# A hybrid mixer layer on one core: the output projection with pairs of token tiles, seven products of quarters in place of eight

## The chip, the cores and the metric

The kernel runs on one core of a Trainium2 chip. Its time is the device time of one execution in microseconds (us); the times given are those of repeated executions on the same inputs. Five engines work side by side: TensorE (PE: matmuls; PEld is its weight load), VectorE (DVE), ScalarE (ACT), GpSimd (POOL) and SyncE (SP), which here only issues transfers. Each engine runs its own instructions in the order written out for it, and a wait at the head of that order holds back everything behind it.

## The reference

One layer for two requests: a prompt of 128 tokens and a sample of 2048 (2176 in all, 17 tiles of 128), model width 1024. All arithmetic is float32:

```python
xn = rmsnorm(h, ln_g) * (1.0 + scale) + shift
proj = jnp.einsum('btd,de->bte', xn, w_in)            # three mixers, their gates, three merge gates
br = jnp.stack([o_a, o_b, o_c], axis=2)               # delta net, spatial gating, Fourier: 512 wide each
pb = jnp.einsum('btnw,nwd->btnd', br, w_branch)
gt = jax.nn.sigmoid(gates.reshape(B, T, N_BRANCH, D_MODEL))
merged = jnp.einsum('btnd,btnd->btd', gt, pb)
out = jnp.einsum('btd,de->bte', merged, w_out)        # the out-projection
h = h + gate * out                                    # gate: a part of the adaLN modulation
y = rmsnorm(h, final_g)
```

The change touches the last three lines and the loading of `w_out`.

## The kernel before

Every float32 operand of a large product is scaled by a power of two and split in two float16 parts, hi and lo; a product is three matmuls (hi x hi, hi x lo, lo x hi) that accumulate in one PSUM bank. The power of two comes from a sum of squares: ACT squares the operand (L209 for weights, L1464 for merged tiles), DVE casts the sum (L175), PE adds it over the partitions with one matmul of one column against `ones`, DVE makes the scale with five one-column steps (L183 to L187, L220), ACT writes the high part (L222, L1466) and DVE the low part (L223, L1467).

The last part of the program has four stages. merge(1), merge(2) and merge(0) each handle one branch: for eight column blocks of 128 (db 0 to 7) and, in each, token tiles of 512, 512, 128 (upper half) and 512, 512 (lower half), PE computes the gate's 24 matmuls and the branch's 12; ACT takes the sigmoid (L1389), DVE multiplies (L1398), POOL adds onto the merged rows (L1399), which are read from and written back to DRAM (`mrg`: load L1377 on SP, store L1406 on POOL). Weights for the next db are loaded by `read_w` (L195) into the staging buffer `wst`. It has two copies (`bufs=2`), and the gate weights (w_in), W_branch, the adaLN rows for the output gate (`gate_rows`, L1421, summed by DVE on L386) and W_out all go through those two. merge(0) is the last: in it, one block of W_out per db is loaded, scaled by itself, and split into `wohi` and `wolo` by `out_w`.

Then comes the out-projection, 17 token tiles in the order 16, 8 to 15, 0 to 7. `out_prep` (L1453 to L1470) loads a tile of merged rows, squares, scales and splits it, and, since each column block of W_out has its own scale, makes eight inverse scales (L1469) with which POOL scales the gate's row per tile (L1489). Per tile and half of the columns, 24 matmuls (L161: token tile as the stationary operand, 512 columns of W_out as the moving one) fill a bank; DVE multiplies by the gate (L1524), POOL adds the input row (L1525), ACT squares (L1534), POOL takes the power (L171), DVE multiplies by the final norm (L1537), and the row is stored (L1538). PSUM has three banks for these products (`ps_mm`), three others (`ps_d`) served the delta net.

The order on each engine is set by the framework, which moves instructions by priority and by what it expects to be ready; `high_priority` lifts a piece of code over what was written before it. The operands of the first five tiles, `pre`, are made when merge(0)'s last upper half is done (`ahead_out`).

Of the kernel before, what the change touches and what calls it, by code (L numbers as in the profile page):

```python
# [111 lines left out]
def hybrid_flow_kernel(ctx: ExitStack, tc: tile.TileContext, x_prompt, x_sample, state_delta, c, c_ctx, ln_g, w_ada,  # L112
# [1340 lines left out]
    def out_prep(t, pl, tag, hl=None):  # L1453
        mt = sb(pl, [P, KT, P], tag, bufs=2)
        SY.dma_start(mt, mD[:, :, t * P:(t + 1) * P].rearrange("k p t -> p k t"))
        if hl is None:
            mh = sb(orp, [P, KT, P], "mh", F16, bufs=3)
            ml = sb(orp, [P, KT, P], "ml", F16, bufs=3)
        else:
            mh = sb(wp, [P, KT, P], "whi", F16, bufs=4)  # L1460
            ml = sb(wp, [P, KT, P], "wlo", F16, bufs=4)
        ss = sb(orp, [P, 1], "mss", bufs=2)
        with tc.high_priority():
            A.activation(ml, mt, AF.Square, accum_out=ss)  # L1464
# [1 line left out]
            A.activation(mh, mt, AF.Copy, scale=s)  # L1466
            V.scalar_tensor_tensor(ml, mt, s, mh, ALU.mult, ALU.subtract)  # L1467
# [1 line left out]
        V.tensor_scalar(inv8, winv, inv, None, ALU.mult)  # L1469
# [16 lines left out]

    def scale_gate(out, src, inv):
        k = inv.shape[-1]
        G.tensor_tensor(out.rearrange("p (k x) -> p k x", k=k), src.rearrange("p (k x) -> p k x", k=k),  # L1489
                        inv.rearrange("p (k o) -> p k o", o=1).to_broadcast([P, k, P]), ALU.mult)  # L1490
# [18 lines left out]
    part = sb(op, [P, 2], "part", bufs=1)  # L1509
    for i_, t in enumerate(order):  # L1510
        mh, ml, inv8 = pre[i_]
        xr = sb(op, [P, D], "xr")
        SY.dma_start(xr, xrows(t * P, P))
        hh = sb(op, [P, D], "hh")
        if i_:
            gt = sb(op, [P, D], "gt")
            scale_gate(gt, gb, inv8)
        for i in range(2):
            cs = slice(i * 512, (i + 1) * 512)
            ps = bank(ps_mm, [P, 512])  # L1520
            gemm_N(ps, mh, ml, wo, i * 512, 512)
            dst, gc = (hh[:, cs], gt[:, cs]) if i_ else (gp[i], gp[i])
            with tc.high_priority():
                V.tensor_tensor(dst, ps, gc, ALU.mult)  # L1524
            (V if i_ == 16 else G).tensor_tensor(hh[:, cs], dst, xr[:, cs], ALU.add)  # L1525
# [4 lines left out]
        ss2 = sb(op, [P, 1], "hss")  # L1530
        if i_ == 16:
            G.tensor_tensor(ss2, part[:, 0:1], part[:, 1:2], ALU.add)
        else:
            A.activation(xr, hh, AF.Square, accum_out=ss2)  # L1534
        rsqrt(ss2, ss2, 1.0 / D, 1)
        for cs in ([slice(0, 512), slice(512, D)] if i_ == 16 else [slice(0, D)]):
            V.scalar_tensor_tensor(hh[:, cs], hh[:, cs], ss2, fg[:, cs], ALU.mult, ALU.mult)  # L1537
# [28 lines left out]
```

## Time and profile before

| | us |
|---|---|
| three executions: median (lowest, highest) | 2190.88 (2185.53, 2194.47) |
| the profiled execution: its time | 2189.41 |
| its span on the core | 2187.6 |
| PE, DVE, ACT, POOL busy | 2123.6, 1320.9, 1015.0, 701.6 |
| mean granted TensorE clock | 0.991 of full speed |
| first and last matmul of the out-projection | 2002.71, 2179.43 |

Times in the rows count from the start of the span. A row of the groups reads: line, engine, operation, output <- inputs by the program's names with partitions x elements, x count, then busy us and mean ns of one, then the idle time ahead of them and what ended it. A row of the timeline reads: start, duration, engine, line, operation, names, and in brackets the idle time before it. PE's matmuls overlap, so the distance between two starts tells what one costs.

### The profile page before, as it was taken

The page shows a single profiled execution, that of the slowest core. Times are in us where ns is not written, and L with a number is a line of the kernel's source. Part 1 is how long each engine was busy: PE and PEld are TensorE (multiplying, and loading weights), DVE is VectorE, ACT ScalarE, POOL GpSimd, SP SyncE. Part 2 cuts the span into 40 slices and gives each one's busy share as a digit, 9 for nine tenths or more (in the row PEclk, how much of TensorE's full clock was granted, in tenths as well). Part 3 has the DMA queues.
Part 4 walks back from the last instruction along what each step waited for, and adds up shares of the span by engine and source line. Part 5 has one row for each costly group of instructions (what it writes and reads, how often), then busy time and mean ns, then how long its engine had stood idle before and what let it go on. Part 6 is the DMA issues. An engine that isn't in the chain of part 4 may idle for free.

```text
span 2187.6 us, 42676 instructions
## 1 busy us (share of the span) xinstructions
PE 2123.6 (97%) x16234; PEld 1214.9 (56%) x16234; DVE 1320.9 (60%) x3150; ACT 1015.0 (46%) x2355; POOL 701.6 (32%) x862
## 2 busy tenths in 40 slices
PE   7999999999999998999899999999999999999998
PEld 3565444455555587878555556555554444444443
DVE  5746854469879698776665555765663544323454
ACT  3644744345566474554544445655543422222332
POOL 1421333223334324322312223344432221222543
PEclk9999999999999999999999999999999999999999
DMA  8424823167777664544655555766654544324542
GB/s 282 141 87 148 290 95 106 61 204 222 253 232 240 198 197 139 146 121 127 197 183 157 174 160 180 242 196 203 198 173 150 174 129 129 116 78 127 173 148 103
DMA packets 304727, 365.09 MB, mean 167 GB/s; under 512 B 39585, under 2 KB 215946, under 8 KB 302474
## 3 DMA queue, kind: packets, MB, share of 16 engines
q1 hardware_dynamic: 289386, 302.19, 45.4%
q0 software_dynamic: 12688, 51.27, 6.5%
q10 hardware_dynamic: 2448, 8.91, 1.0%
q8 instruction: 127, 2.08, 0.4%
q14 instruction: 78, 0.64, 0.1%
HBM read 234.67 MB, written 127.62 MB: 166 GB/s over the span
## 4 chain that ended last, share of the span: by engine, by line
PE 50%; DMA 4%; DVE 4%; ACT 1%; issue 1%; POOL 0%; SPq 0%; DVEq 0%; POOLq 0%; ACTq 0%
PE b L161 50%; DMA st<-br 1%; DMA ES<-ei 1%; DMA mrg<-mrow 1%; DMA wst<-in_w_in_dram 0%; DVE XB L797 0%; DVE E L798 0%; DVE big L1360 0%; DMA mrow<-mrg 0%; DMA S<-in_state_delta_dram 0%; DMA wst<-in_w_branch_dram 0%; PE b L1057 0%; ACT big L1359 0%; DMA sq__2210_18514<-qT 0%; DMA qk<-n 0%
## 5 line engine op out<-in xcount | busy, mean ns | idle before, releaser
L161 PE MATMUL b<-xh,whi 128*128 128x512 f16 (+1 forms) x1920 | 652.6, 349 | 1.4 <-DVE mrow L1395 1.0
L161 PE MATMUL b<-xl,whi 128*128 128x512 f16 (+1 forms) x1920 | 652.9, 349 | 0.0
L161 PE MATMUL b<-xh,wlo 128*128 128x512 f16 (+1 forms) x1920 | 651.6, 348 | 0.0
L161 PEld LDWEIGHTS <-whi 128*128 128x128 f16 x3904 | 358.1, 98 | 329.2 <-issue 10.2
L161 PEld LDWEIGHTS <-wlo 128*128 128x128 f16 x1952 | 191.6, 98 | 179.0 <-issue 3.6
L161 PE MATMUL b<-big,bhi 128*128 128x512 f16 (+1 forms) x960 | 249.7, 347 | 1.4 <-ACT big L1359 1.1
L1399 POOL TENSOR_TENSOR mrow<-mrow,sg 128x512 f32<-128x512 f32 (+1 forms) x80 | 92.6, 1158 | 282.9 <-DVE sg L1398 220.5
L161 PE MATMUL b<-big,blo 128*128 128x512 f16 (+1 forms) x480 | 163.1, 347 | 0.0
L1389 ACT ACTIVATE sg<-b,winv 128x512 f32<-128x512 f32 (+1 forms) x120 | 74.2, 618 | 172.0 <-PE b L161 171.1
L161 PEld LDWEIGHTS <-xh 128*128 128x128 f16 x1496 | 117.7, 98 | 28.0
L161 PEld LDWEIGHTS <-bhi 128*128 128x128 f16 x960 | 86.9, 98 | 75.6
L1398 DVE SCALAR_TENSOR_TENSOR sg<-b,binv,sg 128x512 f32<-128x512 f32 (+1 forms) x80 | 53.4, 667 | 121.4 <-PE b L161 118.7
L646 POOL TENSOR_TENSOR cy<-cy,raw 128x545 f32<-128x545 f32 (+1 forms) x48 | 66.4, 1408 | 185.7 <-ACT raw L645 185.7
L175 DVE CAST wscb<-wss 128x1 bf16<-128x1 f32 x93 | 14.3, 154 | 154.5 <-ACT wlo L209 71.4
L866 POOL COPY T<-ES 32x256 f16<-32x256 f16 x68 | 31.0, 456 | 220.1 <-DMA ES<-ei 217.6
L161 PE MATMUL b<-whi,xh 128*128 128x128 f16 x544 | 94.0, 220 | 0.0
L161 PE MATMUL b<-wlo,xh 128*128 128x128 f16 x544 | 93.9, 220 | 0.0
L161 PE MATMUL b<-whi,xl 128*128 128x128 f16 x544 | 93.8, 220 | 0.0
L161 PE MATMUL b<-wohi,mh 128*128 128x512 f16 x240 | 90.9, 379 | 1.3 <-ACT mh L1466 1.3
L161 PE MATMUL b<-wohi,ml 128*128 128x512 f16 x240 | 90.8, 379 | 0.3 <-DVE mscb L175 0.3
L161 PE MATMUL b<-wolo,mh 128*128 128x512 f16 x240 | 90.9, 379 | 0.0
L209 ACT ACTIVATE wlo<-wst 128x1024 f16<-128x1024 f32 x52 | 54.9, 1056 | 77.4 <-DMA wst<-in_w_in_dram 75.5
(456 smaller groups left out, 4298.1 us busy)
## 6 DMA issues: line engine op xcount, KB each, us to landing
wst<-in_w_in_dram SPq DMA_DIRECT2D x60, 512.0 KB
qkv<-cy POOLq DMA_DIRECT2D x12, 1089.0 KB, 5.2
st<-br SPq DMA_DIRECT2D x48, 256.0 KB
mrow<-mrg SPq DMA_DIRECT2D x18, 512.0 KB
mrow<-mrg SPq DMA_DIRECT2D x16, 576.0 KB
mrg<-mrow POOLq DMA_DIRECT2D x16, 576.0 KB, 3.6
dc<-dec SPq DMA_DIRECT2D x17, 512.0 KB
kq<-qkv SPq DMA_DIRECT2D x34, 256.0 KB
```

What stands on the lines that cost most here:

```text
L161: PE.matmul(out, l, r, start=start, stop=stop)
L175: V.tensor_copy(sb16, ss)
L209: A.activation(w.lo, st, AF.Square, accum_out=ss)
L646: G.tensor_tensor(y[:, c0:c1], y[:, c0:c1], raw[:, 1 + c0:1 + c1], ALU.mult)
L866: G.tensor_copy(T16[rows(a0, b), :, :, b], ES[0:32, :, 2 * a0 + b, :, wT])
L1389: A.activation(sg, ps, AF.Sigmoid, scale=gw.inv)
L1398: V.scalar_tensor_tensor(sg, ps, binv[:, 1:2], sg, ALU.mult, ALU.mult)
L1399: G.tensor_tensor(mr, mr, sg, ALU.add)
```

## The change

A merged matrix of 256 tokens (a pair of tiles) by 1024, times W_out of 1024 by 1024, is split in quarters: each side 2 x 2. Instead of eight products of quarters, seven are formed from sums of quarters and combined by additions (the Winograd form of Strassen's scheme). One product of quarters is 4 x 3 matmuls of 128 tokens by 512 columns. Tile 16, the odd one, is done alone as before.

- All of W_out now has one scale. `out_weights`, a generator of which `merge` takes one step per token tile, reads the eight blocks of W_out twice: first for the squares only (L1461), then for the high and low parts. Two steps per block then make the sixteen quarter sums (four sums n by four column blocks j): three, two or two TENSOR_TENSORs on DVE, a cast on ACT, the low part on DVE, and a store to DRAM (`tw`, L1507, 256 KB each). These pieces are pinned with `keep_in_program_order`.
- After the last gate product, `tw` is read back into the place of `xh` (L1591, four loads of 1 MB).
- `pair_sums` (two squares on ACT, one common scale, four sums of quarters on POOL) runs two pairs ahead, `pair_operands` (high and low parts of seven quarters, in `xl`) one pair ahead, in steps between the products of the current pair.
- Per pair, two banks are copied by ACT, five are joined by DVE with an earlier sum, and DVE gates the four results (one factor per token now, so that POOL no longer scales the gate's row). POOL does two sums and four additions, DVE the four additions of the last pair. The banks come from `ps_mm` and `ps_d` in turn, six in all.
- The eight inverse scales and the per-tile gate rows are gone.

```diff
@@ -1359,7 +1359,7 @@
             A.activation(o16[:, 0, g, t0:t0 + tn], st, AF.Copy, scale=s)
             V.scalar_tensor_tensor(o16[:, 1, g, t0:t0 + tn], st, s, o16[:, 0, g, t0:t0 + tn], ALU.mult, ALU.subtract)
-    def merge(n, first, inv, each=None, halves=HALVES, mid=None, then=None):
+    def merge(n, first, inv, each=None, halves=HALVES, mid=None, then=None, work=iter(())):
         steps, sinv = iter(()), None
         for db in range(KT):
@@ -1398,6 +1398,7 @@
                             V.scalar_tensor_tensor(sg, ps, binv[:, 1:2], sg, ALU.mult, ALU.mult)
                         G.tensor_tensor(mr, mr, sg, ALU.add)
                     pace.tick(tn * MT)
+                    next(work, 0)
                     if sinv is not None:
                         for _ in steps:
                             pass
@@ -1444,98 +1445,269 @@
-    winv = sb(orp, [P, KT], "winv8")
-    def out_w(i):
-        w = load_w(w_out[0][:, i * P:(i + 1) * P], KT, hi=whi[:, :, i * P:(i + 1) * P], lo=wlo[:, :, i * P:(i + 1) * P])
-        V.tensor_mul(winv[:, i:i + 1], w.inv, sx)
...
+    wos = sb(orp, [P, KT + 1], "wos")
+    twD = dram("tw", [P, 4, 4, 1024], F16)
+    wsc = []
+    def block(i):
+        return read_w(w_out[0][:, i * P:(i + 1) * P], KT)
+    def out_weights():
+        kept = tc.keep_in_program_order
+        st = None
+        for i in range(KT + 1):
+            last, st = st, block(i) if i < KT else None
+            if last is not None:
+                kept(A.activation(sb(orp, [P, KT, P], "t16", F16, bufs=2), last, AF.Square, accum_out=wos[:, i - 1:i]))
+            yield
+        kept(V.tensor_reduce(wos[:, KT:KT + 1], wos[:, 0:KT], AX.X, ALU.add))
+        wsc.extend(scales(wos[:, KT:KT + 1], orp, "osc"))
+        s = wsc[0]
+        order_, ready = [0, 4, 1, 5, 2, 6, 3, 7, None, None], []
+        b_, st = None, None
+        for i in range(10):
+            prev, last, b_, st = b_, st, order_[i], block(order_[i]) if order_[i] is not None else None
+            if last is not None:
+                hi, lo = [w_[:, :, prev * P:(prev + 1) * P] for w_ in (whi, wlo)]
+                kept(A.activation(hi, last, AF.Copy, scale=s))
+                kept(V.scalar_tensor_tensor(lo, last, s, hi, ALU.mult, ALU.subtract))
+                if prev > 3:
+                    ready.extend((n, prev - 4) for n in range(4))
+            for _ in range(2):
+                if ready:
+                    quarter_sum(*ready.pop(0))
+                yield
+        while ready:
+            quarter_sum(*ready.pop(0))
+            yield
+    tf_ = []
+    def quarter_sum(n, j):
+        kept = tc.keep_in_program_order
+        quarter = lambda kk, cc: [w_[:, 4 * kk:4 * kk + 4, (4 * cc + j) * P:(4 * cc + j + 1) * P] for w_ in (whi, wlo)]
+        b11, b12, b21, b22 = [quarter(kk, cc) for kk in range(2) for cc in range(2)]
+        if not tf_:
+            tf_.append(sb(orp, [P, 4, P], "tf"))
+        tf = tf_[0]
+        if n < 2:
+            (ah, al), (bh, bl) = (b12, b11) if n == 0 else (b22, b12)
+            kept(V.tensor_tensor(tf, ah, bh, ALU.subtract))
+            kept(V.tensor_tensor(tf, tf, al, ALU.add))
+            kept(V.tensor_tensor(tf, tf, bl, ALU.subtract))
+        elif n == 2:
+            for x_ in b11:
+                kept(V.tensor_tensor(tf, tf, x_, ALU.add))
+        else:
+            kept(V.tensor_tensor(tf, b21[0], tf, ALU.subtract))
+            kept(V.tensor_tensor(tf, tf, b21[1], ALU.add))
+        t16 = sb(orp, [P, 2, 4, P], "t16", F16, bufs=2)
+        kept(A.copy(t16[:, 0], tf))
+        kept(V.tensor_tensor(t16[:, 1], tf, t16[:, 0], ALU.subtract))
+        SY.dma_start(twD[:, n, j], t16.rearrange("p l k c -> p (l k c)"))
...
+    def m_scale(mts):
+        jk = sb(orp, [P, KT, P], "t16", F16, bufs=2)
+        ss = sb(orp, [P, 3], "mss", bufs=2)
+        for i, mt in enumerate(mts):
+            A.activation(jk, mt, AF.Square, accum_out=ss[:, i:i + 1])
+        if len(mts) > 1:
+            V.tensor_add(ss[:, 2:3], ss[:, 0:1], ss[:, 1:2])
+        s, inv = scales(ss[:, 2:3] if len(mts) > 1 else ss[:, 0:1], orp, "msc")
+        minv = sb(orp, [P, 1], "minv", bufs=3)
+        V.tensor_mul(minv, inv, wsc[1])
+        return s, minv
+    def halved(hi, lo, src, s):
+        A.activation(hi, src, AF.Copy, scale=s)
+        V.scalar_tensor_tensor(lo, src, s, hi, ALU.mult, ALU.subtract)
...
+    def pair_sums(a, b):
+        s, minv = m_scale([a, b])
+        yield
+        sf = sb(orp, [P, 4, 4, P], "sf")
+        a11, a12, a21, a22 = a[:, 0:4], a[:, 4:8], b[:, 0:4], b[:, 4:8]
+        G.tensor_tensor(sf[:, 0], a21, a22, ALU.add)
+        G.tensor_tensor(sf[:, 1], sf[:, 0], a11, ALU.subtract)
+        G.tensor_tensor(sf[:, 2], a11, a21, ALU.subtract)
+        G.tensor_tensor(sf[:, 3], a12, sf[:, 1], ALU.subtract)
+        summed.append((a, b, sf, s, minv))
+    def pair_operands(i, a, b, sf, s, minv):
+        v = xl.rearrange("p k t -> p (k t)")[:, (i % 2) * 7168:(i % 2 + 1) * 7168].rearrange("p (l s k c) -> p l s k c", l=2, s=7, k=4)
+        operands.append((v, minv))
+        halved(v[:, 0, 0:2].rearrange("p s k c -> p (s k) c"), v[:, 1, 0:2].rearrange("p s k c -> p (s k) c"), a, s)
+        yield
+        halved(v[:, 0, 2], v[:, 1, 2], b[:, 4:8], s)
+        yield
+        for h in (slice(0, 2), slice(2, 4)):
+            halved(v[:, 0, 3:7][:, h], v[:, 1, 3:7][:, h], sf[:, h], s)
+            yield
...
+    PAIRS = [(t, t + 1) for t in list(range(8, 16, 2)) + list(range(0, 8, 2))]
-            for i, t in enumerate(order[:5]):
+            pre.append(out_single(16))
+            run(pair_sums(*[m_load(t, wp, "wst") for t in PAIRS[0]]))
...
-    merge(0, False, inv_, tail, HALVES[::-1], ahead_out)
+    merge(0, False, inv_, tail, HALVES[::-1], ahead_out, work=out_weights())
     ms_.close()
...
+    tw = xh.rearrange("p k t -> p (k t)")[:, 0:16384].rearrange("p (n j l k c) -> p n j l k c", n=4, j=4, l=2, k=4)
+    for n in (2, 0, 1, 3):
+        SY.dma_start(tw[:, n].rearrange("p j l k c -> p j (l k c)"), twD[:, n])
+    with tc.high_priority():
+        run(pair_operands(0, *summed[0]))
...
-    for i_, t in enumerate(order):
-        mh, ml, inv8 = pre[i_]
...
-            ps = bank(ps_mm, [P, 512])
-            gemm_N(ps, mh, ml, wo, i * 512, 512)
-            dst, gc = (hh[:, cs], gt[:, cs]) if i_ else (gp[i], gp[i])
-            with tc.high_priority():
-                V.tensor_tensor(dst, ps, gc, ALU.mult)
-            (V if i_ == 16 else G).tensor_tensor(hh[:, cs], dst, xr[:, cs], ALU.add)
-            if i_ == 16:
-                A.activation(xr[:, cs], hh[:, cs], AF.Square, accum_out=part[:, i:i + 1])
-        if i_ < 12:
...
+    def raw(kk, cc):
+        return lambda l, k: (whi, wlo)[l][:, 4 * kk + k, 512 * cc:512 * cc + 512]
+    def mixed(n):
+        return lambda l, k: tw[:, n, :, l, k, :]
+    L, R = slice(0, 512), slice(512, D)
+    for i_, (ta, tb) in enumerate(PAIRS):
+        end = i_ == len(PAIRS) - 1
+        v, minv = operands[i_]
+        def coming():
+            if i_ + 2 < len(PAIRS):
+                nx = [m_load(t, op, "mt") for t in PAIRS[i_ + 2]]
+            if not end:
+                yield from pair_operands(i_ + 1, *summed[i_ + 1])
+            if i_ + 2 < len(PAIRS):
+                yield from pair_sums(*nx)
+        ahead_ = coming()
+        ha, hb = rows_of(ta), rows_of(tb)
+        part = sb(op, [P, 2], "part")
...
+        def formed(slot, w, even):
+            ps = bank(ps_mm if even else ps_d, [P, 512])
+            for k in range(4):
+                mm(ps, v[:, 0, slot, k, :], w(0, k), k == 0, False)
+                mm(ps, v[:, 0, slot, k, :], w(1, k), False, False)
+                mm(ps, v[:, 1, slot, k, :], w(0, k), False, k == 3)
+            next(ahead_, 0)
+            return ps
...
+        u1 = kept(formed(0, raw(0, 0), True))
+        u2 = joined(temp(), formed(4, mixed(2), False), u1)
+        c11 = joined(u1, formed(1, raw(1, 0), True), u1)
+        gated(c11, c11, L)
+        added(ha, c11, L)
+        u5 = kept(formed(3, mixed(0), False))
+        u3 = joined(temp(), formed(5, mixed(1), True), u2)
+        G.tensor_tensor(u2, u2, u5, ALU.add)
+        E2.tensor_tensor(u5, u3, u5, ALU.add)
+        gated(u5, u5, R)
+        added(hb, u5, R)
+        c12 = joined(u2, formed(6, raw(1, 1), False), u2)
+        gated(c12, c12, R)
+        added(ha, c12, R)
+        final(ha, ta)
+        c21 = joined(u3, formed(2, mixed(3), True), u3)
+        gated(c21, c21, L)
+        added(hb, c21, L)
+        if end:
+            A.activation(jk[:, R], hb[:, R], AF.Square, accum_out=part[:, 1:2])
+            A.activation(jk[:, L], hb[:, L], AF.Square, accum_out=part[:, 0:1])
+        final(hb, tb, part if end else None)
+        run(ahead_)
```

**How the rows move.** ACT, from the first gate tiles of db 1 in merge(0), before (`sg` is a sigmoid; `wolo`, `wlo`, `blo` are squares of W_out, the gate weights and W_branch; `wohi`, `whi`, `bhi` their high parts):

```order
L1389 ACTIVATE sg_23276<-b_23251,winv_22972 128x512
L209 ACTIVATE blo_23450,wss_23451<-wst_23339 128x512
L222 ACTIVATE bhi_23449<-wst_23339,wsc_23501 128x512
L1389 ACTIVATE sg_23322<-b_23297,winv_22972 128x512
L1389 ACTIVATE sg_23377<-b_23352,winv_22972 128x128
L1389 ACTIVATE sg_23432<-b_23407,winv_22972 128x512
L209 ACTIVATE wolo_23214,wss_23516<-wst_23514 128x8x128
L209 ACTIVATE wlo_23579,wss_23580<-wst_23495 128x1024
L222 ACTIVATE wohi_23213<-wst_23514,wsc_23522 128x8x128
L1389 ACTIVATE sg_23478<-b_23453,winv_22972 128x512
```

and in the changed kernel:

```order
L1389 ACTIVATE sg_23307<-b_23282,winv_22972 128x512
L1461 ACTIVATE t_2833_23339,wos_23215<-wst_23280 128x1024
L209 ACTIVATE blo_23443,wss_23444<-wst_23324 128x512
L1389 ACTIVATE sg_23366<-b_23341,winv_22972 128x128
L222 ACTIVATE bhi_23442<-wst_23324,wsc_23498 128x512
L1389 ACTIVATE sg_23425<-b_23400,winv_22972 128x512
L1461 ACTIVATE t_2838_23387,wos_23215<-wst_23337 128x1024
L1461 ACTIVATE t_2847_23448,wos_23215<-wst_23385 128x1024
L209 ACTIVATE wlo_23562,wss_23563<-wst_23492 128x1024
L1389 ACTIVATE sg_23475<-b_23450,winv_22972 128x512
L1461 ACTIVATE t_2857_23507,wos_23215<-wst_23446 128x1024
L1461 ACTIVATE t_2868_23567,wos_23215<-wst_23505 128x1024
```

Squares of four blocks of W_out (L1461) stand where the square and the high part of one stood, and the gate weights' square comes behind two of them.

SP, the loads at the same place, before (`mrow` are merged rows):

```order
L195 DMA wst_23339<-in_w_branch_dram 128x4x128
L195 DMA wst_23495<-in_w_in_dram 128x8x128
L195 DMA wst_23514<-in_w_out_dram 128x8x128
L1377 DMA mrow_23532<-mrg 128x1152
L1421 DMA wst_23534<-in_w_ada_dram 128x4x256
L195 DMA wst_23624<-in_w_branch_dram 128x4x128
L195 DMA wst_23780<-in_w_in_dram 128x8x128
```

and in the changed kernel:

```order
L195 DMA wst_23324<-in_w_branch_dram 128x4x128
L195 DMA wst_23337<-in_w_out_dram 128x8x128
L1377 DMA mrow_23515<-mrg 128x1152
L195 DMA wst_23385<-in_w_out_dram 128x8x128
L195 DMA wst_23446<-in_w_out_dram 128x8x128
L195 DMA wst_23492<-in_w_in_dram 128x8x128
L195 DMA wst_23505<-in_w_out_dram 128x8x128
L1422 DMA wst_23517<-in_w_ada_dram 128x4x256
L1377 DMA mrow_23677<-mrg 128x1024
L195 DMA wst_23565<-in_w_out_dram 128x8x128
L195 DMA wst_23611<-in_w_branch_dram 128x4x128
```

Between two loads of W_branch there were three loads into `wst`; there are now seven.

SP at the passage from merge(0) to the out-projection, in the changed kernel (`xh<-tw` is the read-back, `mt` the merged tiles of pair 1 and then of pair 2, `hh` input rows):

```order
L1377 DMA mrow_25439<-mrg 128x1024
L1591 DMA xh_93<-tw 128x4096 x4
L1598 DMA hh_25543<-in_x_prompt_dram 128x1024
L1603 DMA gb_25545<-gate 128x1024
L1605 DMA fg_25547<-in_final_g_dram 128x1024
L1511 DMA mt_25550<-mrg 128x8x128
L1511 DMA mt_25552<-mrg 128x8x128
L1598 DMA hh_25635<-in_x_sample_dram 128x1024
L1598 DMA hh_25637<-in_x_sample_dram 128x1024
L1511 DMA mt_25653<-mrg 128x8x128
L1511 DMA mt_25655<-mrg 128x8x128
```

The read-back stands ahead of everything that the pairs load; before, only the loads of merged tiles and input rows were there.

More of the change, by code (lines that the diff above doesn't have):

```diff
@@ L1472, in hybrid_flow_kernel @@
-    pre, gp = [], []
+    wos = sb(orp, [P, KT + 1], "wos")
[31 more added lines that the diff above has]
+            yield
@@ new lines, in m_load @@
+    def m_load(t, pl, tag):
+        mt = sb(pl, [P, KT, P], tag, bufs=4 if tag == "mt" else 2)
+        SY.dma_start(mt, mD[:, :, t * P:(t + 1) * P].rearrange("k p t -> p k t"))
+        return mt
+    def m_scale(mts):
[9 more added lines that the diff above has]
+        return s, minv
@@ L1474, in half_gate, with run @@
+    def run(gen):
+        for _ in gen:
+            pass
+    summed, operands = [], []
+    gp, pre = [], []
     def half_gate(i):
@@ L1507, in hybrid_flow_kernel @@
     SY.dma_start(fg, final_g[None, :].to_broadcast([P, D]))
-    part = sb(op, [P, 2], "part", bufs=1)
-    for i_, t in enumerate(order):
-        mh, ml, inv8 = pre[i_]
[L1512 to L1519, printed above, removed]
-            ps = bank(ps_mm, [P, 512])
-            gemm_N(ps, mh, ml, wo, i * 512, 512)
-            dst, gc = (hh[:, cs], gt[:, cs]) if i_ else (gp[i], gp[i])
-            with tc.high_priority():
-                V.tensor_tensor(dst, ps, gc, ALU.mult)
-            (V if i_ == 16 else G).tensor_tensor(hh[:, cs], dst, xr[:, cs], ALU.add)
-            if i_ == 16:
-                A.activation(xr[:, cs], hh[:, cs], AF.Square, accum_out=part[:, i:i + 1])
-        if i_ < 12:
-            pre.append(out_prep(order[i_ + 5], op, "mt"))
+    jk = sb(op, [P, D], "ojk", F16, bufs=1)
@@ L1530, in hybrid_flow_kernel, with final @@
+    def final(hh, t, sq=None):
         ss2 = sb(op, [P, 1], "hss")
-        if i_ == 16:
-            G.tensor_tensor(ss2, part[:, 0:1], part[:, 1:2], ALU.add)
+        if sq is None:
+            A.activation(jk, hh, AF.Square, accum_out=ss2)
         else:
-            A.activation(xr, hh, AF.Square, accum_out=ss2)
+            V.tensor_add(ss2, sq[:, 0:1], sq[:, 1:2])
         rsqrt(ss2, ss2, 1.0 / D, 1)
-        for cs in ([slice(0, 512), slice(512, D)] if i_ == 16 else [slice(0, D)]):
+        for cs in ([slice(0, D)] if sq is None else [slice(0, 512), slice(512, D)]):
@@ L1537, in hybrid_flow_kernel @@
             V.scalar_tensor_tensor(hh[:, cs], hh[:, cs], ss2, fg[:, cs], ALU.mult, ALU.mult)
             SY.dma_start(y_sample[0, t * P:(t + 1) * P, cs] if t < 16 else y_prompt[0, :, cs], hh[:, cs])
+    loaded = [m_load(t, op, "mt") for t in PAIRS[1]]
+    mh, ml, minv = pre[0]
+    wo = _W()
+    wo.hi, wo.lo = whi, wlo
+    for i in range(2):
+        cs = slice(i * 512, (i + 1) * 512)
+        ps = bank(ps_mm, [P, 512])
+        gemm_N(ps, mh, ml, wo, i * 512, 512)
+        with tc.high_priority():
+            V.scalar_tensor_tensor(gp[i], ps, minv, gp[i], ALU.mult, ALU.mult)
+        G.tensor_tensor(h16[:, cs], gp[i], h16[:, cs], ALU.add)
@@ new lines, in hybrid_flow_kernel, with gated, added, temp @@
+    final(h16, 16)
+    run(pair_sums(*loaded))
+    def raw(kk, cc):
[16 more added lines that the diff above has]
+        part = sb(op, [P, 2], "part")
+        def gated(dst, src, cs):
+            with tc.high_priority():
+                V.scalar_tensor_tensor(dst, src, minv, gb[:, cs], ALU.mult, ALU.mult)
+        E2 = V if end else G
+        def added(hh, src, cs):
+            E2.tensor_tensor(hh[:, cs], src, hh[:, cs], ALU.add)
+        def temp():
+            return sb(ep, [P, 512], "sg", bufs=4)
+        def formed(slot, w, even):
[6 more added lines that the diff above has]
+            return ps
+        def kept(ps):
+            t = temp()
+            with tc.high_priority():
+                A.copy(t, ps)
+            return t
+        def joined(dst, ps, other):
+            with tc.high_priority():
+                V.tensor_tensor(dst, ps, other, ALU.add)
+            return dst
+        u1 = kept(formed(0, raw(0, 0), True))
[21 more added lines that the diff above has]
+        run(ahead_)
```

37 lines of the change are left out of this document (11 added, 26 removed).

## The prediction

> **What bounds the kernel now.** First the page (its first part, then the granted clock by slice), then PE's waits in the last stages, then two stretches by windows: 1750 to 1800 us lies in the last merge, 2006 to 2178 in the out-projection (columns: busy PE, PEld, DVE, ACT, POOL, then clock, DMA share, GB/s).
>
> ```profile
> PE 2123.6 (97%) x16234; PEld 1214.9 (56%) x16234; DVE 1320.9 (60%) x3150; ACT 1015.0 (46%) x2355; POOL 701.6 (32%) x862
> PEclk9999999999999999999999999999999999999999
> ...
> GB/s 282 141 87 148 290 95 106 61 204 222 253 232 240 198 197 139 146 121 127 197 183 157 174 160 180 242 196 203 198 173 150 174 129 129 116 78 127 173 148 103
> ```
> ```profile
> PE b L161 <- ACT mh L1466: 1.3, 1, 1.3
> PE b L161 <- DVE mscb L175: 0.3, 1, 0.3
> ```
> ```profile
> 1750.00:1800.00 50.00, 50.00 (x280) 24.31 (x278) 21.04 (x57) 13.90 (x22) 10.40 (x11) 1.00 0.42 133
> ...
> 2006.00:2178.00 172.00, 172.00 (x811) 78.17 (x810) 86.50 (x170) 51.06 (x75) 81.35 (x67) 1.00 0.46 152
> ```
>
> TensorE is busy for all of both stretches, at full clock. The two waits are all that PE has from 1660 us to the end. So a matmul taken out of the out-projection is worth its whole pitch, and a wait that anything else puts before PE costs its whole length. Nothing else is near its limit: DVE and POOL stand at 50% and 47% there.
>
> ```profile
> 2002.71 0.39 PE L161 MATMUL b<-wohi,mh 128*128 128x512 f16 x1 [1.30 <-ACT mh L1466]
> ...
> 2179.43 0.38 PE L161 MATMUL b<-wohi,ml 128*128 128x512 f16 x1
> ```
>
> These are the first and the last of the 816 matmuls of 512 columns: (2179.43 - 2002.71) / 815 = 0.2168 us each, scale sums included.
>
> **Removed: 96 matmuls.** Before, 17 tiles x 2 halves x 24 = 816. After, tile 16 alone has 48, and eight pairs have seven products of 12, so 84 each: 720. 96 x 0.2168 = 20.8 us. A pair then lasts 84 x 0.2168 = 18.2 us.
>
> **Does a pair stay on PE?** Prices for the other engines, from the groups of 2006 to 2188:
>
> ```profile
> L1525 POOL TENSOR_TENSOR hh<-hh,xr 128x512 f32<-128x512 f32 x30 | 38.0, 1267 | 74.0 <-DVE hh L1524 44.8 <-issue 24.6 <-DVE msc L187 4.5
> L1524 DVE TENSOR_TENSOR hh<-b,gt 128x512 f32<-128x512 f32 x32 | 22.0, 687 | 26.0 <-PE b L161 22.8 <-POOL gt L1489 3.0 <-DMA out_dram<-hh 0.2
> L1537 DVE SCALAR_TENSOR_TENSOR hh<-hh,hss,fg 128x1024 f32<-128x1024 f32 x16 | 21.5, 1346 | 14.0 <-POOL hss L171 14.0
> L1534 ACT ACTIVATE xr<-hh 128x1024 f32<-128x1024 f32 x16 | 16.9, 1056 | 31.9 <-POOL hh L1525 31.8
> L1467 DVE SCALAR_TENSOR_TENSOR ml<-mt,msc,mh 128x1024 f16<-128x1024 f32 x12 | 15.4, 1283 | 3.0 <-ACT mh L1466 3.0
> L1466 ACT ACTIVATE mh<-mt,msc 128x1024 f16<-128x1024 f32 x12 | 13.8, 1147 | 41.2 <-DVE msc L186 41.2
> L1469 DVE TENSOR_SCALAR inv<-winv,msc 128x8 f32<-128x8 f32 x15 | 11.9, 792 | 0.5
> L171 POOL TENSOR_TENSOR hss<-hss,mhalf 128x1 f32<-128x1 f32 x17 | 9.3, 550 | 1.8 <-DVE hss L170 1.8
> ```
>
> DVE per pair: low halves of seven slots (3.5 x 1.283 = 4.5), five joins and four gatings (9 x 0.687 = 6.2), two finals (2.7), about ten one-column steps of 0.15 (1.5): 14.9 of 18.2. POOL: four sums of operands and six additions (10 x 1.267) and two powers: 13.8. ACT: high halves 4.0, two copies of a bank (1.3, at a half of L1466's rate), four squares (4 x 1.24 with the read-out): 10.3. All fit, with six banks of slack, so I take 18.2. Bounds: L1469, a tiny step that does the same every time, averages 792 ns where POOL works; three steps so stretched give DVE 16.8, still under 18.2. The new moving operand, a quarter sum, is four runs of 128 columns. Its lower bound is the same pitch, its upper that of four 128-column matmuls, 0.055 each by the rows below: 0.22 against 0.2168, or 1.3 us over 384 of them. I take none. The quarter sums' read-back, 4.2 MB at the page's best 290 GB/s, is 14.5 us; it is issued when the last gate product frees `xh`, 2.6 us (12 matmuls) before the merge ends, and its first quarter is wanted 60 matmuls (13.0 us) after: hidden.
>
> **Start and end.** Tile 16's operands no longer stand behind a sigmoid and a further tile's square: the 1.3 us wait above goes, less 0.1. Pair 2's loads stand on SP behind the read-back, the rows of tile 16 and pair 0, two broadcasts and pair 1's loads, and PE's one-column sum for them sits inside pair 1, some 28 us after the merge: 0.5 us late (0 to 3). At the end before, the chain after the last matmul was
>
> ```profile
> 2179.85 0.70 DVE hh L1524
> ...
> 2183.21 0.75 DVE hh L1537
> ```
>
> After it, a join stands before the gating (0.7) and the other tile's final (1.35) goes ahead on DVE: 2.0 to 2.6, so 2.3. Out-projection: -20.8 - 1.2 + 0.5 + 2.3 = -19.2.
>
> **Added: W_out is read twice, through the two staging buffers** that the gate weights, W_branch and the adaLN rows use too. That is the term that decides. Before, around db 1 of the last merge:
>
> ```profile
> 1765.89 0.37 SPq L1421 DMA_DIRECT2D wst<-in_w_ada_dram  x1
> 1767.44 0.37 SPq L195 DMA_DIRECT2D wst<-in_w_branch_dram  x1
> 1773.25 0.37 SPq L195 DMA_DIRECT2D wst<-in_w_in_dram  x1
> ...
> 1777.93 0.37 SPq L195 DMA_DIRECT2D wst<-in_w_out_dram  x1
> ```
> ```profile
> 1771.13 0.63 ACT L209 ACTIVATE blo<-wst 128x512 f16<-128x512 f32 x1 [5.04 <-DMA wst<-in_w_branch_dram]
> ...
> 1781.67 1.06 ACT L209 ACTIVATE wolo<-wst 128x1024 f16<-128x1024 f32 x1 [1.07 <-DMA wst<-in_w_out_dram]
> ```
> ```profile
> 1769.62 2.07 DVE L386 SCALAR_TENSOR_TENSOR sg<-wst,scT,sg 128x256 f32<-128x256 f32 x5 [1.55 <-DMA wst<-in_w_ada_dram]
> 1771.89 0.16 DVE L175 CAST wscb<-wss 128x1 bf16<-128x1 f32 x1 [0.19 <-ACT blo L209]
> 1771.96 1.27 DVE L386 SCALAR_TENSOR_TENSOR sg<-wst,scT,sg 128x256 f32<-128x256 f32 x3
> ```
> ```profile
> 1782.24 0.22 PE L161 MATMUL b<-xh,whi 128*128 128x128 f16 x1
> 1782.30 0.22 PE L161 MATMUL b<-xl,whi 128*128 128x128 f16 x1
> ```
>
> A load is used 3.7 us after its issue (1767.44 to 1771.13, 1777.93 to 1781.67; the adaLN rows 1765.89 to 1769.62). In the changed order SP has, one behind another on the two buffers, W_out, W_out, gate weights, W_out, adaLN rows, W_out, and only then W_branch for db 2, each waiting for the step that reads the buffer two before it. From 1759.8, when the first of these can issue (a merged row stands ahead of it): its load and square (3.7 + 1.25, with the read-out), the gate weights' load, their square, a sigmoid and the second block's square (3.7 + 1.25 + 0.7 + 1.25), the third block's load and square (4.95), together 16.8; with one more issue 1777.0. The adaLN rows are there at 1780.8, their eight sums and a multiplication (2.07 + 1.27 + 0.75) end at 1784.9, W_branch lands at 1788.7, its square and cast are done at 1789.7. PE wants that scale ten or more matmuls into the 128-column tile that began at 1782.24, at 1783.8 with 0.7 lost just before: it waits **5.9 us**. Before, the same load was in use at 1771.13, 11 us ahead of its need. In db 5 the gate weights stand behind W_branch, behind a merged row that waits for POOL's store, and a gate multiplication behind the quarter sums on DVE: 3 us (0 to 5). Smaller ones in db 1 and 3: 0.7 + 0.5. Together 10.1. Below, none of it is lost if loads overlap more than this chain; above, as much again in db 2 to 4.
>
> The ACT copies and DVE sums of the quarters themselves (16 x about 4 steps of 128x512, 40 us of DVE) lie in 200 us in which DVE is 42% busy: hidden but for the order.
>
> **A stall also costs clock.** The trace has one like it, at 1539.9, where PE lacked work for 1.76 us:
>
> ```profile
> 1541.67 0.29 PE L161 MATMUL b<-v,R 128*128 128x128 f16 x2 [1.76 <-DVE wsc L186]
> ...
> 1543.45 0.63 PE L161 MATMUL b<-xh,whi 128*128 128x512 f16 x1
> 1543.88 0.63 PE L161 MATMUL b<-xl,whi 128*128 128x512 f16 x1
> ```
> ```profile
> 1542.00:1543.00 1.00, 0.59 (x6) 0.59 (x7) 0.49 (x2) 0.83 (x1) 0.00 (x0) 0.63 0.62 226
> 1543.00:1544.00 1.00, 1.00 (x9) 0.72 (x7) 1.00 (x1) 0.00 (x0) 0.00 (x0) 0.50 0.02 6
> 1544.00:1545.00 1.00, 1.00 (x4) 0.32 (x3) 1.00 (x5) 0.00 (x0) 0.00 (x0) 0.50 0.00 0
> 1545.00:1546.00 1.00, 1.00 (x9) 0.44 (x8) 0.78 (x2) 0.18 (x1) 0.58 (x1) 0.66 0.44 83
> ```
>
> The clock then stood at 0.63, 0.50, 0.50, 0.66, and matmuls came 0.43 us apart: 0.37 + 0.50 + 0.50 + 0.34 = 1.7 us lost. I charge it for the two long stalls: 3.4. [...]
>
> **Sum.** -19.2 + 10.1 + 3.4 = -5.7 against the profiled 2189.41 (span 2187.6 and 1.8 around it). The median is 1.47 above that run: 2190.88 - 5.7 = **2185.2**, 0.26% less. One per mille is 2.2 us, and about 0.5% (11 us) is what this kernel's measurement can tell from no change.
>
> **Rivals.**
> 1. *The merge stays fed* (0.30). DMA is busy only 42% in the merge, so loads could overlap and the stalls shrink to the small ones: -19.2 + 1.5 gives 2173. Against it: two buffers, each freed by a use, are an order and not a bandwidth.
> 2. *The chain repeats* (0.18). db 2, 3 and 4 carry the second pass of W_out and the first quarter sums; a stall of 3 + 1.7 in each adds 14: 2199. Against it: the adaLN rows, the slowest link, are loaded only twice more.
> 3. *DVE and POOL exclude one another in the pairs* (0.08): slower. If every DVE step that reads two operands from SBUF (4.5 + 2.7 + four gatings 2.7 = 9.9) had to wait while POOL works (13.8), a pair would last 23.7 instead of 18.2, 8 x 5.5 = 44 more: 2229. It decides above 20.3 a pair, where 8 x 2.1 has made up for the forecast's gain and 11 more. L1469 speaks for it; against it, L1467 has two such operands and keeps 1283 ns with POOL at 47%. [...]
> [...]
>
> The forecast has 0.38, with an own range of 2177 to 2194.
>
> **How the numbers follow.** Faster by over 0.5% is below 2179.9: rival 1 nearly whole (0.27) and the forecast's lower part (0.08): 0.35. Slower is above 2201.8: rival 3 and the upper part of rival 2 (0.06): 0.14. The rest, 0.51, is no change. The range leaves out rival 3 and the ends of 1 and 2: 2170 to 2201.
>
> **What would show it.** A wait of PE on the W_branch scale of 4 to 8 us near 1784, with the clock at 0.5 for some 3 us after; a second near db 5; none in pairs 2 to 7, with 18.2 us from pair to pair and POOL and DVE near 80%. The out-projection from first to last matmul should take 156 to 158 us. Wrong if PE in the merge shows no wait over 1 us (rival 1), or if pairs are over 19 us (rival 3).

## The result

The changed kernel takes 2212.89 us (median; 2208.93 to 2215.41), the kernel before, in the same runs, 2190.39: a ratio of 1.0098, 95% interval 1.0078 to 1.0117. It is slower by 1%, outside the range of the prediction, and the rival that had a chance of 0.08 is what happened. The profiled execution took 2213.85 (span 2211.8). Its page, and PE's waits from 1700 us to the end:

```profile
PE 2112.1 (95%) x16123; PEld 1210.2 (55%) x16123; DVE 1421.4 (64%) x3176; ACT 1043.1 (47%) x2403; POOL 768.6 (35%) x888
```
```profile
PE b L161 <- DVE sg L1685: 16.5, 7, 4.0
PE b L161 <- DVE wscb L175: 7.8, 3, 5.3
PE b L161 <- ACT sg L1389: 2.3, 1, 2.3
```

Before, PE waited 1.6 us in all from 1660 us on. Now it waits 16.5 us for the joins of the pairs (L1685: a product's PSUM bank is free for the next one when DVE has joined it) and 10.6 us in the last merge (7.8, 2.3 and 0.6 for a smaller one). Four points in time split the span, for every kernel that was run: the last sigmoid of merge(0), the first and the last matmul of the out-projection, the end.

| | last sigmoid | first to last matmul | end after it | span |
|---|---|---|---|---|
| before | 2000.94 | 176.72 | 8.17 | 2187.6 |
| changed | 2013.80 | 181.58 | 14.42 | 2211.8 |
| difference | +12.9 | +4.9 | +6.3 | +24.2 |

The remaining 0.2 lies between the sigmoid and the first matmul. So 96 matmuls fewer made the out-projection not 20 us shorter but 5 longer.

**The merge** lost about what the sum said. The wait in db 1 (PE's timeline, then windows with the clock in the ninth column of figures, counted as in the prediction):

```profile
1788.03 0.16 PE L161 MATMUL b<-wscb,ones 128*128 128x1 bf16 x1 [5.29 <-DVE wscb L175]
```
```profile
1788.00:1789.00 1.00, 0.97 (x11) 0.97 (x11) 0.60 (x1) 1.00 (x2) 0.00 (x0) 0.50 0.00 0
...
1791.00:1792.00 1.00, 1.00 (x3) 0.30 (x2) 0.83 (x2) 0.00 (x0) 0.09 (x1) 0.50 1.13 325
1792.00:1793.00 1.00, 1.00 (x4) 0.40 (x3) 0.00 (x0) 0.00 (x0) 0.69 (x2) 0.64 0.56 169
```

Its place, its length and the half clock behind it are those forecast, with 5.3 us for 5.9 and 2.4 us of lost clock (4 x 0.5 + 0.36) for 1.7.

The last sigmoid is a point in time, and merge(0) began 1.3 us earlier in the changed kernel (its first product of 512 columns at 1732.21, before at 1733.50), behind stages whose code is the same in both. From its first to its last such product merge(0) takes 282.5 us, before 267.5. So the stage itself lost 15.0 us: 8.6 in db 1, 4.1 in db 3 and 2.4 in db 5. In db 3 PE waited 2.3 us for a sigmoid (the last row of ACT below) that stood behind the cast of a quarter sum and the high part of a block of W_out, and the clock cost 1.7 us more:

```profile
1858.53 0.62 ACT L1505 CAST t<-tf 128x512 f16<-128x512 f32 x1 [8.43 <-issue]
1859.05 1.14 ACT L1472 ACTIVATE wohi<-wst,osc 128x1024 f16<-128x1024 f32 x1
1860.10 0.93 ACT L1389 ACTIVATE sg<-b,winv 128x512 f32<-128x512 f32 x2
```
```profile
1860.82 0.27 PE L161 MATMUL b<-big,bhi 128*128 128x128 f16 x2 [2.26 <-ACT sg L1389]
```

**The pairs** are where the forecast broke. A pair takes 21.3 us (from the first pair matmul at 2027.2 to the last, 2197.4, by eight), not 18.2. Groups of DVE and POOL between 2050 and 2190, then DVE, POOL and PE side by side in a pair (timeline):

```profile
L1663 POOL TENSOR_TENSOR hh<-sg,hh 128x512 f32<-128x512 f32 x27 | 46.5, 1733 | 18.4 <-DVE sg L1658 15.9 <-DVE hss L170 1.8 <-DVE minv L1523 0.6
L1658 DVE SCALAR_TENSOR_TENSOR sg<-sg,minv,gb 128x512 f32<-128x512 f32 x26 | 29.7, 1150 | 1.3 <-POOL sg L1696 1.2
L1616 DVE SCALAR_TENSOR_TENSOR hh<-hh,hss,fg 128x1024 f32<-128x1024 f32 x12 | 22.4, 1868 | 9.6 <-POOL hss L171 9.6
L1685 DVE TENSOR_TENSOR sg<-b,sg 128x512 f32<-128x512 f32 x31 | 21.1, 681 | 3.3 <-POOL sg L1695 3.0
```
```profile
2082.65 1.75 DVE L1658 SCALAR_TENSOR_TENSOR sg<-sg,minv,gb 128x512 f32<-128x512 f32 x1
2084.33 0.68 DVE L1685 TENSOR_TENSOR sg<-b,sg 128x512 f32<-128x512 f32 x1
2084.93 1.90 DVE L1528 SCALAR_TENSOR_TENSOR xl<-sf,msc,xl 128x1024 f16<-128x1024 f32 x1
...
2086.82 0.68 DVE L1685 TENSOR_TENSOR sg<-b,sg 128x512 f32<-128x512 f32 x1
```
```profile
2078.70 1.26 POOL L1546 TENSOR_TENSOR sf<-mt,sf 128x512 f32<-128x512 f32 x1
2079.92 3.94 POOL L1663 TENSOR_TENSOR hh<-sg,hh 128x512 f32<-128x512 f32 x2
2084.49 1.26 POOL L1663 TENSOR_TENSOR hh<-sg,hh 128x512 f32<-128x512 f32 x1 [0.63 <-DVE sg L1658]
```
```profile
2087.55 0.59 PE L161 MATMUL b<-wohi,xl 128*128 128x512 f16 x1 [3.63 <-DVE sg L1685]
```

The gating (L1658), two operands in SBUF, takes 0.74 us where POOL is idle and up to 1.84 where POOL works, 1.15 on average; the final (L1616) 1.28, or about 2.28. POOL's additions take 1.26, 1.7 or 2.25. The join (L1685), one operand in PSUM, is 0.67 to 0.69 in every one of its rows in that stretch. The rows show how this reaches PE: a gating and a low half (L1528, 1.28 alone) that take 1.75 and 1.90 stand ahead of the join at 2086.82, with which a wait of PE of 3.6 us ends. In the end the last pair's chain of these steps adds 6.3 us.

### The profile page after: what moved, and what is told of

It is laid out like the page before. It is cut to its first block, busy times and chain, and to the rows that moved or that the text cites. A ratio compares the mean times of both kernels' runs of the same rounds, so it can differ in the third digit from the quotient of the medians.

```text
span 2211.8 us, 42623 instructions
## 1 busy us (share of the span) xinstructions
PE 2112.1 (95%) x16123; PEld 1210.2 (55%) x16123; DVE 1421.4 (64%) x3176; ACT 1043.1 (47%) x2403; POOL 768.6 (35%) x888
## 5 line engine op out<-in xcount | busy, mean ns | idle before, releaser
L161 PEld LDWEIGHTS <-whi 128*128 128x128 f16 x3840 | 353.4, 98 | 330.7 <-issue 18.3
L161 PEld LDWEIGHTS <-xl 128*128 128x128 f16 x1488 | 140.1, 99 | 117.0 <-issue 25.9
L1399 POOL TENSOR_TENSOR mrow<-mrow,sg 128x512 f32<-128x512 f32 (+1 forms) x80 | 99.9, 1250 | 291.2 <-DVE sg L1398 236.2
L646 POOL TENSOR_TENSOR cy<-cy,raw 128x545 f32<-128x545 f32 (+1 forms) x48 | 75.3, 1597 | 181.1 <-ACT raw L645 181.1
L223 DVE SCALAR_TENSOR_TENSOR wlo<-wst,wsc,whi 128x1024 f16<-128x1024 f32 x52 | 70.7, 1364 | 35.6 <-ACT whi L222 35.6
L161 PE MATMUL b<-xh,xl 128*128 128x512 f16 x384 | 87.5, 380 | 3.4 <-DVE sg L1685 2.5
```

Source lines behind the costliest of these rows:

```text
L161: PE.matmul(out, l, r, start=start, stop=stop)
L223: V.scalar_tensor_tensor(w.lo, st, s, w.hi, ALU.mult, ALU.subtract)
L646: G.tensor_tensor(y[:, c0:c1], y[:, c0:c1], raw[:, 1 + c0:1 + c1], ALU.mult)
L1399: G.tensor_tensor(mr, mr, sg, ALU.add)
```

## The experiments

Two theories for the pairs: **shared access** (a DVE step with two SBUF operands and a POOL addition take turns) and **load only** (DVE simply has too many steps in a bad order); later a third, **late operands**. For the merge: **staging chain** (the first reading of W_out holds up W_branch's load) against **quarter sums**. Up to the last table each run is one execution, and 17 executions of the kernel before spread from 2184.5 to 2198.8 us, so these runs are compared by stages of their traces and only roughly by their times.

**The disputed cost by itself.** Behind the last row of the kernel before (the calls in their order, several to a line):

```diff
+    stt(4, 1024); stt(4, 512); tt_psum(4)      # DVE alone: two SBUF operands; then one of them in PSUM
+    both(); on_pool(4)                         # POOL alone: additions of 128x512
+    both(); on_pool(6); stt(6, 1024)           # side by side
+    both(); on_pool(8); stt(8, 512)
+    both(); on_pool(8); tt_psum(8)
```

> The kernel before, with a piece added behind its last row, in which DVE and POOL work on tiles in SBUF first apart and then side by side. Theory 'shared access': a DVE step that reads two operands from SBUF and a POOL addition take turns. Then six pairs of a 128x1024 step (1.28 alone) and a POOL addition of 128x512 (1.27 alone) side by side take their sum, about 15 us, eight of the 128x512 step (0.75) with eight additions about 16 us, and a DVE step with one operand in PSUM stays at 0.68. Rival 'load only': the engines do not touch each other, and the stretches last 7.7 and 10.2 us, as long as the longer of the two alone.

DVE's timeline (L1558 two SBUF operands, L1562 one in PSUM), then POOL's; a row holds the whole run of equal steps:

```profile
2190.53 8.40 DVE L1558 SCALAR_TENSOR_TENSOR xa<-xb,hss 128x1024 f32<-128x1024 f32 x8
2198.96 2.87 DVE L1562 TENSOR_TENSOR xa<-b,xb 128x512 f32<-128x512 f32 x4
...
2208.81 12.49 DVE L1558 SCALAR_TENSOR_TENSOR xa<-xb,hss 128x1024 f32<-128x1024 f32 x6
...
2222.72 12.42 DVE L1558 SCALAR_TENSOR_TENSOR xa<-xb,hss 128x512 f32<-128x512 f32 x8
...
2236.56 5.75 DVE L1562 TENSOR_TENSOR xa<-b,xb 128x512 f32<-128x512 f32 x8
```
```profile
2202.11 5.28 POOL L1554 TENSOR_TENSOR xd<-xc 128x512 f32<-128x512 f32 x4
...
2207.49 11.40 POOL L1554 TENSOR_TENSOR xd<-xc 128x512 f32<-128x512 f32 x6
...
2221.52 13.07 POOL L1554 TENSOR_TENSOR xd<-xc 128x512 f32<-128x512 f32 x8
...
2235.36 10.66 POOL L1554 TENSOR_TENSOR xd<-xc 128x512 f32<-128x512 f32 x8
```

Alone, an addition is 1.32 and a large and a small DVE step together 2.10 (1.28 and 0.74 by the trace of the kernels, overlaps not counted). Six of each side by side last 13.8 us (2207.49 to 2221.30), 0.88 of the sum 6 x (1.28 + 1.32) = 15.6; eight small ones 13.6, 0.83 of 16.5. They nearly take turns, though short of the full 15 and 16 us. With one operand in PSUM, DVE keeps 0.72 each and POOL 1.33: no touch. Shared access is there. For a pair, the 9.9 and 13.8 us of the prediction's third rival make 19.7 to 20.9 by these rates; 21.3 was measured.

**Without POOL's additions,** all ten or the four operand sums:

```diff
-        G.tensor_tensor(sf[:, 0], a21, a22, ALU.add)      # and the three others (both runs)
-            E2.tensor_tensor(hh[:, cs], src, hh[:, cs], ALU.add)      # these three in the first run alone
-        G.tensor_tensor(u2, u2, u5, ALU.add)
-        E2.tensor_tensor(u5, u3, u5, ALU.add)
```

> The changed kernel without the ten POOL additions of each pair (sums of operands, sums of products, input rows: left out of the computation); DVE, ACT and PE have all their steps. 'Shared access': the gatings fall from 1.15 to 0.75 and the finals from 1.87 to 1.28 on average, PE's waits in the pairs (some 16 us) go, and the out-projection takes 157 to 161 us from first to last matmul instead of 181.6; the time falls to about 2190. 'Load only' (DVE has too many steps in a bad order): DVE's steps and PE's waits stay, 176 us or more, time over 2207.

> The changed kernel with only the four POOL sums of operands per pair left out (their products are formed from plain quarters instead); six additions of ten stay. 'Shared access': an effect in between, 165 to 173 us from first to last matmul. 'Load only': 176 or more. A third, 'late operands' (the pair's operands come too late because they wait for these sums): as short as without all ten, 157 to 161.

First to last matmul: 160.1 us without ten, 159.2 without four; the spans are 2175.8 and 2190.4 (the first also loses the additions of the end, which is then 2.9 us). Groups of the first (L1652 is its gating, L1610 its final), then of the second:

```profile
L1652 DVE SCALAR_TENSOR_TENSOR sg<-sg,minv,gb 128x512 f32<-128x512 f32 x28 | 20.8, 748 | 5.4 <-ACT sg L1674 5.2
L1610 DVE SCALAR_TENSOR_TENSOR hh<-hh,hss,fg 128x1024 f32<-128x1024 f32 x12 | 15.3, 1280 | 0.9 <-POOL hss L171 0.8
```
```profile
L1652 DVE SCALAR_TENSOR_TENSOR sg<-sg,minv,gb 128x512 f32<-128x512 f32 x28 | 26.2, 943 | 1.8 <-POOL sg L1690 1.7
L1610 DVE SCALAR_TENSOR_TENSOR hh<-hh,hss,fg 128x1024 f32<-128x1024 f32 x14 | 19.9, 1423 | 6.6 <-POOL hss L171 6.4
```

DVE had every step of the pairs (the last pair's additions apart), and was fast as soon as POOL was still: load only falls. From the third pair on, a pair takes 18.1 to 18.2 us. But the second run missed its expectation of 165 to 173. DVE is still held up there (0.94 and 1.42), and PE waits only 3.0 us after its first matmul: with six additions a pair DVE has slack enough. That looks like a threshold, but no run lies between six and nine additions a pair. Taken alone it fits late operands as well, since the sums left out were those that make operands.

**All sums kept, fewer steps with two SBUF operands.** In the first, the join goes back into its PSUM bank, so that the gating reads PSUM; in the second, moreover, the final does:

```diff
-        c11 = joined(u1, formed(1, raw(1, 0), True), u1)
-        gated(c11, c11, L)
+        b1 = inplace(formed(1, raw(1, 0), True), u1)      # and so for the other three
+        gated(u1, b1, L)
@@ second @@
-            V.scalar_tensor_tensor(hh[:, cs], hh[:, cs], ss2, fg[:, cs], ALU.mult, ALU.mult)
+                A.activation(ps, hh[:, c_], AF.Copy, scale=ss2)
+                V.tensor_tensor(hh[:, c_], ps, fg[:, c_], ALU.mult)
```

> The changed kernel with the same sums, but the joins of four products with an earlier sum are written back into their PSUM bank, so that the gating reads one operand from PSUM and one from SBUF; ACT copies one more bank, and POOL does nine additions for ten. 'Shared access', by the measured side-by-side rate (two steps take 0.88 of their sum): per pair the DVE steps with two SBUF operands are 4.5 + 2.6 = 7.1, POOL 12.5, together 17.2 where it was 21.0; so the pairs are back on PE at 18.2, and the out-projection takes 157 to 164 us from first to last matmul. 'Late operands' (the POOL sums delay the operands by their own length): the sums are all there, so over 176. Time by the first: about 2190 to 2196 (the merge's loss stays).

> As the one with the joins in place, and in addition the last scaling of each row is done by ACT into PSUM, from where DVE multiplies by the norm's row. Per pair 4.5 + 12.5 = 17.0, times 0.88 = 15.0 on the shared access. 'Shared access': 156 to 160 us from first to last matmul, 1 to 4 less than with the joins alone; 'late operands': over 176.

First to last matmul: 176.1 and 163.7 us; times 2204.1 and 2192.8. Groups of the first (L1658 gating, L1616 final), then of the second (L1662, L1620):

```profile
L1616 DVE SCALAR_TENSOR_TENSOR hh<-hh,hss,fg 128x1024 f32<-128x1024 f32 x14 | 22.7, 1625 | 8.2 <-POOL hss L171 7.9
...
L1658 DVE SCALAR_TENSOR_TENSOR sg<-b,minv,gb 128x512 f32<-128x512 f32 x27 | 20.1, 745 | 1.7 <-POOL sg L1698 1.4
```
```profile
L1662 DVE SCALAR_TENSOR_TENSOR sg<-b,minv,gb 128x512 f32<-128x512 f32 x28 | 20.7, 747 | 4.4 <-POOL sg L1702 4.1
...
L1620 DVE TENSOR_TENSOR hh<-b,fg 128x512 f32<-128x512 f32 x28 | 18.9, 685 | 2.8 <-ACT b L1619 2.7
```

The gating is 0.745 us throughout, as alone. The second run has all four sums and 163.7 us, so late operands falls too; it missed its own range of 156 to 160, with 4.0 us of waits and 3.4 of lost clock. The first got 5.5 us of the 18 to 24 expected: the sum of 17.2 a pair, under 18.2, was not enough. Its finals and low halves were still stretched, and its PE waits (11.6 us) were for ACT's copy of a bank, which waited for a join on DVE. Working the shared access out as one more engine with a load is too kind: it does not count that a held-up step stands ahead of a join that PE needs.

**One reading of W_out.** The first reading is cut to one block, or spread:

```diff
-            last, st = st, block(i) if i < KT else None
+            last, st = st, block(i) if i < 1 else None        # first run
             yield
+            if i < 7:
+                yield                                         # second run: all blocks, two tiles apart
```

> The changed kernel with the first reading of W_out cut from eight blocks to one (the common scale is worked out from that block alone); the second reading, the quarter sums and the pairs stay. Theory 'staging chain': the merge loses its 5.3 us wait in db 1 and the half-rate stretch behind it, so the last sigmoid comes at 2003 to 2006 instead of 2013.8, and the time falls by 8 to 11 us. Rival 'quarter sums': the loss lies in the DVE and ACT steps of the sums, and the last sigmoid stays after 2011.

> The changed kernel with the first reading of W_out spread over 16 tiles of the last merge instead of 9 (two steps without work between its loads); all work is kept. 'Staging chain': W_branch's load in db 1 has fewer loads ahead of it, its wait of 5.3 us shrinks to under 2.5, and the last sigmoid comes at 2001 to 2008 instead of 2013.8; the pairs stay at 181 us. 'It is the number of loads': 2011 or later.

The last sigmoid comes at 2000.83 in the first, with the quarter sums all done; the products take 181.6 us as ever, the time is 2200.6. Spread, all loads kept: 2007.74, products 181.2, time 2207.3. These points in time mislead, though, for merge(0) began at 1728.30 in the first run and at 1735.83 in the second. From its first to its last product it takes 273.1 and 272.5 us, that is 5.6 and 5.0 over the kernel before, where the changed kernel lost 15.0. So the two remedies are worth the same, some 10 us, and both take away the wait in db 1: for that part, two thirds of the loss, the staging chain is the cause, and it was how densely the loads were set: spread, as many of them cost nothing there. The other third stays. With one reading it is the waits in db 3 and 5 again (2.3 us and its clock, 1.6 us); spread, it is 2.6 + 1.7 us of waits in db 5 and 6, for sigmoids and gate products that stand behind W_out's steps and the quarter sums on ACT and DVE. There the rival has its share; the second reading and the sums were not taken apart.

**Both remedies together,** and two variants of the end (the last pair's finals without PSUM; in the first of them also the first tile's final of every pair):

> Joins in place, the last scaling through PSUM and the spread reading together, all work kept. If both causes are right their gains add: last sigmoid at 2001 to 2008, 157 to 160 us for the products, an end of 9 to 12 us, in sum a time of 2171 to 2183, 0.3 to 0.9% under the kernel before. If pairs or merge were slow for another reason, it is slower than 2195.

> As the combined kernel, but the last scaling goes through PSUM only for the second tile of a pair, and for neither tile of the last pair. The end after the last matmul loses the extra ACT step: 9 to 10.5 us instead of 11.7. The two PE waits for the scaling's PSUM bank (2.8 us) shrink to under 1. Against it, one DVE step per pair with two SBUF operands comes back: 4.5 + 1.3 + 12.5 = 18.3, times 0.88 = 16.1, still under 18.2, so no new waits. Time 2180 to 2185 if 'shared access' holds by that sum; if PE waits in the pairs come back, 2188 or more.

> As the combined kernel, with the last pair alone scaled without PSUM: only the end changes, 9 to 10.5 us instead of 11.7, time 2183 to 2187.

| | time | ratio to before, 95% | merge(0): start, first to last product | last sigmoid | first to last matmul | end |
|---|---|---|---|---|---|---|
| together | 2186.83 | 0.9982, 0.9969 to 0.9995 | 1732.85, 271.6 | 2003.90 | 163.4 | 11.7 |
| first tile's final without PSUM too | 2186.15 | 0.9986, 0.9974 to 0.9998 | 1731.13, 273.9 | 2004.52 | 165.7 | 10.2 |
| last pair's finals alone | 2184.48 | 0.9968, 0.9956 to 0.9979 | 1736.32, 271.4 | 2007.09 | 163.6 | 10.2 |

All three are faster than the kernel before, by 0.1 to 0.3%; the intervals of the first two end just under 1. The forecasts of 2171 to 2183 and 2180 to 2185 missed for these two, the third came in its range. In the first, 163 us, not 157 to 160, were left for the products: over the 156.1 of the matmuls PE still waits 3.7 us, for tile 16's low parts and for the scaling's PSUM bank, and loses 3.5 us of clock behind these waits. The second has one more step with two SBUF operands per pair and 2 us more over the out-projection; its waits for the scaling's bank did not shrink under 1 us, they are 4.0 in all where the first has 2.8. The last sigmoid of the third comes 3.2 us later than that of the first because its merge(0) began 3.5 us later. That the last is faster than the first is not shown, as their intervals overlap; what the traces show is the end, 1.5 us shorter.

## Why the prediction was wrong

Term by term, in the prediction's own order:

- **96 matmuls, 20.8 us.** Right: 720 x 0.2168 = 156.1, and the run without POOL's additions took 160.1, with 2.6 us of waits behind the first matmul and 1.7 of lost clock.
- **A pair stays on PE** (taken as 0): the step that failed, 25.5 us (181.6 against 156.1), of which 19.7 are PE's waits from the first matmul on and 4.5 are clock lost behind them; the rest was not traced. The load was counted right: without POOL's additions a pair takes 18.15 us and DVE is busy for 79% of it, 14.3 for 14.9. That DVE and POOL hold one another up was turned down by a misread row. The prediction said of the third rival that L1467 has two SBUF operands and "keeps 1283 ns with POOL at 47%". Two averages over a stage do not say that the two ran at the same moment. In the kernel before, of 22 such steps (L1467, L1537) between 2040 and 2160 just one had a POOL addition beside it:

```profile
2042.85 2.28 DVE L1537 SCALAR_TENSOR_TENSOR hh<-hh,hss,fg 128x1024 f32<-128x1024 f32 x1 [0.41 <-POOL hss L171]
```
```profile
2042.78 1.26 POOL L1525 TENSOR_TENSOR hh<-hh,xr 128x512 f32<-128x512 f32 x1
```

 It took 2.28 us, where the others took 1.28. The price stood in the trace, and the mean of 1346 for L1537, quoted in the prediction, hides it (15 x 1.28 and one 2.28). L1469, which the prediction took as a stretched step, tells the same: it takes 0.23 us where POOL is still, and 0.89 in the nine rows from 2072 to 2156, in each of which it starts inside an addition and ends with it. That a DVE step with one input in PSUM is not touched is what the run with both engines side by side shows (0.72 us alone and beside POOL).
- **The rival's own price,** 23.7 us a pair and 2229, took full turns. By the measured rates it is 19.7 to 20.9, against 21.3. That this comes so near is in part luck: by the same rates the run with the joins in place had 17.2, and its pairs took 20.6.
- **Read-back and strided operand, 0.** Right as far as runs show: no wait on `xh`, and the matmuls on it start 0.217 us apart (twelve in a row of 2.75, with the 0.38 of the last).
- **Start, -1.2.** Wrong: the wait stayed. Tile 16 waited 0.7 and 0.9 us for its operands, in sum as long as before (1.3 and 0.3), and its first matmul came 2.0 us after the last sigmoid, before 1.8.
- **Pair 2's loads, +0.5** (pairs counted from 0). They cost 0.2 us (2045.72). Right behind it PE waited 1.2 us for the high and low parts of pair 1, which the sum did not have.
- **End, +2.3.** It was 6.3: when the last product was done DVE was still behind, waiting for a POOL sum (to 2198.43), and then had a sum, two joins, three gatings and three additions to do before the finals, of which the first tile's stands ahead of the second's. Beside the four additions, one of the two sums of the last pair is on DVE too. POOL holds up none of these steps (0.75 a gating), so this is load that the sum left out.
- **The merge, +10.1 and 3.4 for the clock.** Near in size, 13.5 against 15.0, and right in mechanism for db 1: 8.3 forecast, 8.6 measured, and the chain through two staging buffers made it (one reading less, or a spread one, takes it away). W_branch's load was issued at 1784.28 and PE went on at 1788.03, against 1784.9 and 1789.7 by hand. That the rest comes near is luck: db 5 was given 4.7 and lost 2.4, without half clock; db 3 was given 0.5 and lost 4.1. That the last sigmoid is only 12.9 later owes 1.3 to the earlier start of the stage.

## What to carry to other kernels

Before work is shared out between DVE and POOL, look for moments at which both run with all operands in SBUF, and take the price from those rows: a mean over a stage in which they happen to alternate is the price without contention (here 1.346 us, where the one row with both took 2.28). A DVE step that reads one operand from PSUM was free of it here, so writing a sum back to its bank cost DVE nothing to speak of (0.69 us a join for 0.68) and saved a third of the gating (1.15 to 0.745). It keeps the bank taken for longer, though: PE then waited 11.6 us for the copy that frees one, until the finals were out of the way too. What a second reading through a staging buffer cost here was no matter of bandwidth, for the same loads, spread, cost 10 us less: count the loads between two that PE waits for, each at issue, landing and use. And measure a stage from its own start: a point in time carries along whatever moved ahead of it, here up to 5 us against the kernel before.
